# Finer input loads, identity matmuls and tied weight splits at the first norm, and three re-ordered places behind it

## The chip, the cores and the metric

The kernel runs on one core of a Trainium2 chip. The time is the device time of one execution in microseconds (us); lower is better. The core's engines take instructions from queues of their own, each in order: PE (TensorE, matmuls, with its weight loads shown as PEld), DVE (VectorE), ACT (ScalarE), POOL (GpSimd) and SP (SyncE, which here only issues DMAs). Engines wait for each other by semaphores. The profile also gives the clock that PE was granted (PEclk; 1.00 is full, 0.50 half).

## The reference

640 frames (one prompt of 512, eight streams of 16 new frames) of 1024 channels go through two layers and a final RMSNorm, all in fp32. Layer 0, where nearly all of the change lies, is:

```python
def conv_module(h, hist, g, w_pw1, b_pw1, w_dw, b_dw, ln_g, ln_b, w_pw2, b_pw2):
    a, gate = jnp.split(rms_norm(h, g) @ w_pw1 + b_pw1, 2, axis=-1)
    glu = a * jax.nn.sigmoid(gate)
    full = jnp.concatenate([hist.astype(glu.dtype), glu], axis=1)
    y = depthwise_conv(full, w_dw) + b_dw          # causal, width 31
    y = jax.nn.silu(layer_norm(y, ln_g, ln_b))
    return h + y @ w_pw2 + b_pw2, full[:, -30:]

def swiglu_ffn(h, g, w_in, w_out):
    a, b = jnp.split(rms_norm(h, g) @ w_in, 2, axis=-1)
    return h + (jax.nn.silu(a) * b) @ w_out
```

Layer 1 is chunked attention over 16 heads instead of the convolution, then another FFN of the same form. The last 30 rows of `full` are outputs too.

## The kernel before

Channels lie on the 128 partitions in 8 tiles (k = 0..7), frames along the free dimension in two groups g0 and g1 of 320. Every fp32 product is made of three matmuls on operands split in a high and a low part: `mm3` (L179 to L185) issues wh·xh (L182), wl·xh (L183) and wh·xl (L184). A weight block of 128x2048 is loaded into `raw` (L144, on SP), ACT makes the high part `whi` (L155), DVE or POOL the low part `wlo` (L159). Activations are split by `xsplit`: `xh` on ACT (L171), `xl` on DVE (L172).

A norm squares 8 tiles (L191 on ACT, L194 elsewhere), adds them in order (`acc`, L212), reduces over partitions with a matmul against a column of ones (the mean, L221), adds eps (DVE, `rst`, L255), takes the power -1/2 on POOL (L262), and spreads the row over the partitions with a matmul against the identity matrix (L233). DVE then scales each tile (`n`, L277).

The stages, by time in the profile: first RMSNorm and the pointwise products of the convolution layer with the gate `glu` (L726 to L739) and the depthwise taps, up to 159 us; of the taps some run on DVE (L778), some on ACT and POOL (L785, L788), and some on PE (L832) from copies of a channel tile that are written to DRAM (`sa`, `sb`, L808) and read back shifted (`xa`, `xb`, L814). Then LayerNorm (`conv_ln`, per group: mean, spread, subtract L851, squares and adds L867, spread, scale L883), the product `pw2` with the update of `h` (L924), FFN0 from about 260 us, attention, FFN1 from about 1043 us, final norm.

A scheduler of the framework sets each engine's order from priorities (`high_priority`) and from explicit ties (`tc.issue_after`: not ahead of that instruction). The order of the convolution stage is written out in the string `PLAN` (L69): a letter for a step, a digit for a channel tile; `E7`/`F7` are the products of tile 7 for g0 and g1, `S7 A7` its taps on PE for the first part, `n` the LayerNorm of g0 between the last taps, `m w0 w1` the LayerNorm of g1 and the two `pw2`. `HELD` says how many DVE taps are held back at which step.

In the FFN, seven products of sums stand in for eight (`seven`), with operands `XH`/`XL` per combination (L342, L343). `std` does the first three products plainly, its second half with `XT4` and `X22`, which need the norm of the second half of the frames (`stats(1)`).

Of the kernel before, what the change touches and what calls it, by code (L numbers as in the profile page):

```python
# [15 lines left out]
P = 128  # L16
# [9 lines left out]
SB = 16  # L26
# [10 lines left out]
MEAN_AT, SPREAD_AT, STATS1_AT = 3, 5, 2  # L37
# [7 lines left out]
GAPS = 1, 12, 2  # L45
# [6 lines left out]
C01 = 4  # L52
# [4 lines left out]
SSQ = 'avavavav'  # L57
# [11 lines left out]
SSQ1 = 'ppapappp'  # L69
LNO = ((0, 1, 4, 5, 6, 2, 3, 7), (0, 1, 4, 2, 3, 5, 6, 7))  # L70
PLAN = ("a0 y x1 b0 b1 q0 dp1s0 c2 k ds1p2 D3 C4 S3 q3 ds2 C5 E6 S4 A4 F6 B4 E7 e S5 A5 F7 k k k S6 A6 "
        "S7 A7 n s0 m w0 w1")

HELD = {(1, 0): 21, (2, 0): 9}
# [7 lines left out]
def tile_trunk(ctx, tc, xT, vecs, hist, w_pw1, w_pw2, w_in0, w_out0, w_os0, w_in1, w_out1, w_os1,  # L82
# [28 lines left out]

    def load_x(g):
# [20 lines left out]
    def wsplit(src, k, n, parts=1, pool=0, cuts=1, gains=None):  # L133
# [6 lines left out]
        else:  # L140
            src = src if len(src.shape) == 2 else src.rearrange("p m c -> p (m c)")
            for i in range(cuts):
                a, b = sz * i // cuts, sz * (i + 1) // cuts
                nc.sync.dma_start(raw[:, a:b], src[:, a:b])  # L144
# [7 lines left out]
        with tc.high_priority(offset=HP):  # L152
            for i in range(cuts):
                a, b = sz * i // cuts, sz * (i + 1) // cuts
                nc.scalar.activation(out=hi[:, a:b], in_=raw[:, a:b], func=AF.Copy)  # L155
                c = b - (b - a) * pool // 4
                for eng, a, b in ((nc.vector, a, c), (nc.gpsimd, c, b)):
                    if a < b:
                        eng.tensor_tensor(out=lo[:, a:b], in0=raw[:, a:b],  # L159
                                          in1=hi[:, a:b].bitcast(F32), op=ALU.subtract)  # L160
        return hi, lo

    @contextmanager
    def behind(*ins):
        with ExitStack() as st:
            for i in ins:
                st.enter_context(tc.issue_after(i))
            yield

    def xsplit(src, hi, lo):  # L170
        split_end[0] = nc.scalar.activation(out=hi, in_=src, func=AF.Copy).ins  # L171
        nc.vector.tensor_tensor(out=lo, in0=src, in1=hi.bitcast(F32), op=ALU.subtract)  # L172
# [14 lines left out]
    def square(s, n, eng="a", q=None):  # L187
        if q is None:
            q = tp.tile([P, tw[0]], F32, tag=sqt[0], name=nm("sq"))
        if eng == "a":  # L190
            nc.scalar.activation(out=q[:, :n], in_=s, func=AF.Square)  # L191
# [10 lines left out]
    def colmean(st, pieces, n, cut, tag, eng=nc.gpsimd, accp=None):  # L202
# [3 lines left out]
        for s in pieces[:cut]:  # L206
# [5 lines left out]
            eng.tensor_tensor(out=acc[:, :n], in0=prev, in1=s(), op=ALU.add)  # L212
# [17 lines left out]

    def spread(st, r, n, ins=False):
        for t, a in enumerate(tiles(n)):
            end = nc.tensor.matmul(st[:, a:a + P], r[:, t:t + 1].to_broadcast([P, P]), ident,  # L233
                                   start=True, stop=True)
        return end.ins if ins else st[:, :n]
# [12 lines left out]
    def rstd_bc(pieces, n, engs=SQ, cut=CUT, r2=None, eng=nc.gpsimd, newton=False,  # L248
                accp=None, sqs=None):
# [3 lines left out]
                         for i, (s, e) in enumerate(zip(pieces, engs))], n,  # L253
                       cut, "rst", eng, accp)
        nc.vector.tensor_scalar(out=r[:, :nt], in0=v, scalar1=EPS, scalar2=None,  # L255
                                op0=ALU.add)
# [4 lines left out]
        else:  # L261
            nc.gpsimd.tensor_tensor(out=r2[:, :nt], in0=r[:, :nt], in1=mhalf[:, :nt], op=ALU.pow)  # L262
# [6 lines left out]
    def rms(g, gain, engs=SQ, cut=CUT, eng=nc.gpsimd, hold=None):  # L269
        n = gr[g][1]  # L270
        bc, _ = rstd_bc([hp(g, k) for k in range(KT)], n, engs, cut, None, eng,
                        accp=hold and hold())
        xh, xl = new_xs(g)
        for k in range(KT):
            t = hold() if hold and k < 2 else tp.tile([P, tw[0]], F32, tag="n1", name=nm("n1"),
                                                       bufs=NB1)
            nc.vector.scalar_tensor_tensor(out=t[:, :n], in0=hp(g, k), scalar=col(gain, k),  # L277
                                           in1=bc, op0=ALU.mult, op1=ALU.mult)
# [25 lines left out]
    def ffn(l, w_in, w_out, w_os, tail, hf, lead=(), b0=None):  # L304
# [1210 lines left out]
```

## Time and profile before

| | us |
|---|---|
| median of 3 runs (lowest, highest) | 1488.08 (1486.97, 1489.66) |
| profiled execution | 1485.55 |
| its span from first to last instruction | 1483.6 |
| PE busy | 1429.4 (96%) |
| DVE busy | 1138.3 (77%) |
| ACT busy | 757.2 (51%) |
| PE idle until the first mean (L221) | 12.3 |
| PE idle for `xa` of tile 7 (L832) | 6.1 |

The span is 1.95 us shorter than the time of its execution, and that execution 2.5 us shorter than the median. Idle time of PE is what a change of order can take away; the page's list of waits names, for each, the instruction that waited and the one that released it. A matmul's printed time includes the end of its pipeline; what a stream of them costs is read from start to start.

### The profile page before, as it was taken

Reading aid. Unit: us, or ns where it says so; the run is one execution under the profiler, and the core shown is the slowest. Engines: PE = TensorE matmul, PEld = TensorE weight load, DVE = VectorE, ACT = ScalarE, POOL = GpSimd, SP = SyncE. Lnnn points to the kernel's source line nnn. Section 1 sums busy time; section 2 is a strip of 40 time slices with the busy share of each in tenths; the row PEclk is TensorE's granted clock in tenths of the full one; section 3 lists DMA queues with packets and bytes.
Section 4 is the critical chain, followed back from the end, with each engine's and each line's share of the span. In section 5 each row is a group of like instructions: output and inputs, shape, how many; then the busy total and the mean of one; then the engine's idle time right before and its main releaser. Section 6 shows DMA issues by size and latency. Waiting matters only on the chain.

```text
span 1483.6 us, 28030 instructions
## 1 busy us (share of the span) xinstructions
PE 1429.4 (96%) x10932; PEld 1365.9 (92%) x10932; DVE 1138.3 (77%) x2523; ACT 757.2 (51%) x1620; POOL 297.7 (20%) x356
## 2 busy tenths in 40 slices
PE   5999899999999999999999999999999999999997
PEld 5998699999999999999988888987899999999997
DVE  5789656799888888866766767566799888888755
ACT  3666245465454564445655454443565455455443
POOL 5789102001111111103222112010001111111101
PEclk9999999999999999999999999999999999999999
DMA  7256514125445444433655555361224444544512
GB/s 239 68 160 189 138 58 136 36 75 143 131 116 133 134 118 130 132 109 133 212 164 204 180 173 193 129 208 23 86 75 129 138 118 117 150 118 108 153 64 72
DMA packets 66660, 192.56 MB, mean 130 GB/s; under 512 B 12000, under 2 KB 30176, under 8 KB 58080
## 3 DMA queue, kind: packets, MB, share of 16 engines
q1 hardware_dynamic: 52736, 161.10, 33.5%
q0 software_dynamic: 13504, 29.37, 9.7%
q8 instruction: 86, 1.41, 0.4%
q14 instruction: 46, 0.38, 0.1%
q10 hardware_dynamic: 288, 0.31, 0.1%
HBM read 179.14 MB, written 11.61 MB: 129 GB/s over the span
## 4 chain that ended last, share of the span: by engine, by line
PE 77%; DVE 8%; POOL 6%; ACT 3%; DMA 3%; issue 3%; SPq 0%; POOLq 0%; DVEq 0%; ACTq 0%
PE mm L409 46%; PE mm L182 8%; PE mm L183 7%; PE mm L184 7%; POOL ca L788 5%; PE am L1226 1%; PE am L1209 1%; PE w L221 1%; PE w L1242 1%; ACT whi L147 1%; PE am L1273 1%; DVE wlo L343 1%; PE mm L832 1%; DVE B L446 1%; PE w L1185 1%
## 5 line engine op out<-in xcount | busy, mean ns | idle before, releaser
L409 PE MATMUL mm<-XH,wlo 128*128 128x320 f32 x896 | 276.9, 310 | 0.0
L409 PE MATMUL mm<-XH,whi 128*128 128x320 f32 x896 | 276.1, 311 | 0.7 <-ACT t L419 0.5
L409 PE MATMUL mm<-XL,whi 128*128 128x320 f32 x896 | 274.4, 310 | 0.0
L342 ACT ACTIVATE whi<-raw 128x512 fp32r<-128x512 f32 (+2 forms) x280 | 169.2, 614 | 141.3 <-PE mm L409 116.5
L182 PE MATMUL mm<-xh,whi 128*128 128x320 f32 (+2 forms) x640 | 202.5, 318 | 6.4 <-ACT xh L171 4.2
L343 DVE TENSOR_TENSOR wlo<-raw,whi 128x512 fp32r<-128x512 f32 (+2 forms) x280 | 184.9, 668 | 22.4 <-ACT whi L342 21.0
L183 PE MATMUL mm<-xh,wlo 128*128 128x320 f32 (+2 forms) x640 | 201.1, 315 | 0.6 <-DVE wlo L159 0.6
L184 PE MATMUL mm<-xl,whi 128*128 128x320 f32 (+2 forms) x640 | 198.4, 313 | 0.0
L409 PE MATMUL mm<-hid,whi 128*128 128x320 f32 x732 | 171.4, 310 | 2.2 <-DVE hid L343 2.2
L409 PEld LDWEIGHTS mm<-XH,whi 128*128 128x128 f32 x896 | 168.4, 189 | 2.1 <-ACT t L419 1.3
L409 PEld LDWEIGHTS mm<-XH,wlo 128*128 128x128 f32 x896 | 169.0, 189 | 0.0
L409 PEld LDWEIGHTS mm<-XL,whi 128*128 128x128 f32 x896 | 167.9, 188 | 0.0
L182 PEld LDWEIGHTS mm<-xh,whi 128*128 128x128 f32 x640 | 122.5, 192 | 9.7 <-ACT xh L171 5.0
L409 PEld LDWEIGHTS mm<-hid,whi 128*128 128x128 f32 x732 | 124.8, 188 | 4.2 <-DVE hid L343 3.2
L183 PEld LDWEIGHTS mm<-xh,wlo 128*128 128x128 f32 x640 | 122.9, 192 | 1.0 <-DVE wlo L159 0.8
L184 PEld LDWEIGHTS mm<-xl,whi 128*128 128x128 f32 x640 | 121.8, 191 | 0.4 <-issue 0.2
L409 PE MATMUL mm<-hid,wlo 128*128 128x320 f32 x366 | 112.9, 308 | 0.0
L409 PE MATMUL mm<-XL,shi 128*128 128x320 f32 x344 | 105.5, 308 | 5.0 <-DVE XL L343 5.0
L409 PE MATMUL mm<-XH,shi 128*128 128x320 f32 x344 | 105.8, 308 | 0.7 <-ACT XH L342 0.7
L409 PE MATMUL mm<-XH,slo 128*128 128x320 f32 x344 | 105.7, 307 | 0.0
L388 POOL DMA_DIRECT2D s<-in_w_in x38 | 22.1, 581 | 386.2 <-DVE wlo L343 207.9
L788 POOL TENSOR_TENSOR ca<-ca,cvt 128x512 f32<-128x512 f32 x60 | 91.7, 1528 | 15.0 <-ACT cvt L785 8.0
(255 smaller groups left out, 3345.2 us busy)
## 6 DMA issues: line engine op xcount, KB each, us to landing
raw<-in_w_in SPq DMA_DIRECT2D x38, 1024.0 KB
s<-in_w_in POOLq DMA_DIRECT2D x76, 256.0 KB, 4.2
raw<-in_w_os SPq DMA_DIRECT2D x24, 768.0 KB
cache<-in_ck SPq DMA_DIRECT2D x32, 512.0 KB
cache<-in_cv SPq DMA_DIRECT2D x32, 512.0 KB
raw<-in_w_pw SPq DMA_DIRECT2D x12, 1024.0 KB
s<-in_w_os POOLq DMA_DIRECT2D x48, 192.0 KB, 3.6
raw<-in_w_kq SPq DMA_DIRECT2D x8, 1024.0 KB
```

Of the source, the lines that this page charges most:

```text
L147: nc.scalar.activation(out=hi[:, a:b], in_=raw[:, a:b], func=AF.Copy, scale=gain)
L182: nc.tensor.matmul(ps, wh, xh, start=(first and i == 0), stop=False)
L183: nc.tensor.matmul(ps, wl, xh, start=False, stop=False)
L184: end = nc.tensor.matmul(ps, wh, xl, start=False, stop=(stop and i == last))
L221: mean_end[0] = nc.tensor.matmul(st[:, 512 + t * w + k:513 + t * w + k], s[:, a:a + P], onec, start=True, stop=True).ins
L342: put_end[1] = nc.scalar.activation(out=hi, in_=src, func=AF.Copy).ins
L343: put_end[0] = nc.vector.tensor_tensor(out=lo, in0=src, in1=hi.bitcast(F32), op=sub).ins
L388: nc.gpsimd.dma_start(s1, src[:, 2 * n:3 * n])
L409: last = nc.tensor.matmul(pt, wt, v, start=(first and k == i == 0), stop=(k == n - 1 and i == 2), skip_group_check=True)
L446: nc.vector.scalar_tensor_tensor(out=out, in0=x, scalar=-1.0, in1=y, op0=mult, op1=op)
L788: nc.gpsimd.tensor_tensor(out=acc, in0=acc, in1=pr, op=ALU.add)
L832: conv_end[0] = nc.tensor.matmul(pt[32 * q:32 * q + 32, 0:n], w4[0:r, 4 * tg + q, :], mv, start=(tg == 0), stop=(tg == 7)).ins
```

## The change

At the first norm: the two loads of the first 320 frames become four of two channel tiles each, and so do those of the second; the weight loads of the first tile are put behind the last of them. `warm(n)` issues n matmuls of the 128x128 identity by itself into a product tile: 30 at the start (nothing but `ident` is waited for), 9 behind the mean, 5 behind the spread of g0 and 5 behind that of g1. The splits of the first two weight blocks are tied behind the last square, the last add, `rst`, `pow` or a scaled tile. The last square goes from DVE to ACT; the squares of g1 go all to ACT. The split of weight block 2 is made in two halves.

At the end of the convolution: the store of `sa` stands ahead of the copy to `out_convs`; the second `pw2` block is loaded early, the split of the first is made late (token `f`); the read of `xb` of tile 6 is put behind that of `xa` of tile 7; fewer DVE taps run before F7, the rest behind it. The LayerNorm of g1 is interleaved with the parts of `pw2` of g0 (`GAPS1`).

In the FFNs: the squares of `stats` get eight tiles of their own in place of two rotating ones; in FFN1 the third plain product's second half stands behind the spread, and `stats(1)` is tied one step earlier. At the end of attention the mean and the spread of FFN1's first half stand one half-product later (`MEAN_AT`, `SPREAD_AT`).

PE at the start of the program, before; `w` is the tile of the mean and the spread, `mm` are product tiles, `ident` the identity:

```order
1 L221 MATMUL w_4_119<-onec,acc_122 128x1 x3
2 L233 MATMUL w_4_119<-ident,rst_15_149 128x128 x3
3 L182 MATMUL mm_209<-xh_154,whi_105 128x320
4 L183 MATMUL mm_209<-xh_154,wlo_106 128x320
5 L182 MATMUL mm_234<-xh_154,whi_105 128x320
6 L183 MATMUL mm_234<-xh_154,wlo_106 128x320
7 L182 MATMUL mm_268<-xh_154,whi_190 128x320
```

and of the changed kernel:

```order
1 L145 MATMUL mm_106<-ident 128x128 x30
2 L237 MATMUL w_2_137<-onec,acc_140 128x1 x3
3 L145 MATMUL mm_169<-ident 128x128 x9
4 L251 MATMUL w_2_137<-ident,rst_13_167 128x128 x3
5 L145 MATMUL mm_199<-ident 128x128 x5
6 L198 MATMUL mm_258<-xh_197,whi_180 128x320
7 L199 MATMUL mm_258<-xh_197,wlo_181 128x320
```

Four groups of `ident` products (the fourth is further down, behind the second spread) now stand around the mean and the spread.

SP at the end of the convolution before, from the store of `sb` of tile 6 (`raw` is a weight block of `pw2`):

```order
55 L808 DMA sb_1566<-gall 128x350
56 L144 DMA raw_2403<-in_w_pw 128x2048
57 L814 DMA xb_1568<-sb_1566 32x4x350
58 L814 DMA xb_1568<-sb_1566 32x4x349
59 L814 DMA xb_1568<-sb_1566 32x4x348
60 L814 DMA xb_1568<-sb_1566 32x4x347
61 L957 DMA out_convs<-gall 128x368
62 L808 DMA sa_1672<-gall 128x590
63 L814 DMA xa_1674<-sa_1672 32x4x590
```

and of the changed kernel, from that store:

```order
54 L846 DMA sb_1631<-gall 128x350
55 L846 DMA sa_1726<-gall 128x590
56 L1015 DMA out_convs<-gall 128x368
57 L852 DMA xa_1728<-sa_1726 32x4x590
58 L852 DMA xa_1728<-sa_1726 32x4x589
59 L852 DMA xa_1728<-sa_1726 32x4x588
60 L852 DMA xa_1728<-sa_1726 32x4x587
61 L852 DMA xb_1733<-sb_1631 32x4x350
```

The store of `sa` of tile 7 moved from behind the weight load, the four `xb` reads and `out_convs` to directly behind the store of `sb`, and its reads stand ahead of those of `xb`; the weight load went further ahead.

DVE between the taps and the sums of the LayerNorm of g0, before (`w` are taps, `gall` the gate's output, `y` the convolution's result):

```order
216 L778 SCALAR_TENSOR_TENSOR w_113_789<-gall,dwv,w_113_789 128x128
217 L778 SCALAR_TENSOR_TENSOR w_174_1225<-gall,dwv,w_174_1225 128x128 x13
218 L739 SCALAR_TENSOR_TENSOR gall<-t_226_1836,t_227_1838 128x320
219 L159 TENSOR_TENSOR wlo_2347<-raw_2345,whi_2346 128x2048
220 L212 TENSOR_TENSOR acc_1986<-y_102 128x320
221 L212 TENSOR_TENSOR acc_1986<-acc_1986,y_102 128x320 x5
222 L225 TENSOR_REDUCE mst_1999<-w_233_1985 128x3
```

and of the changed kernel:

```order
215 L816 SCALAR_TENSOR_TENSOR w_178_1285<-gall,dwv,w_178_1285 128x128 x5
216 L777 SCALAR_TENSOR_TENSOR gall<-t_233_1887,t_234_1889 128x320
217 L816 SCALAR_TENSOR_TENSOR w_178_1285<-gall,dwv,w_178_1285 128x128 x4
218 L179 TENSOR_TENSOR wlo_1494<-raw_1492,whi_1493 128x2048
219 L816 SCALAR_TENSOR_TENSOR w_178_1285<-gall,dwv,w_178_1285 128x128 x9
220 L228 TENSOR_TENSOR acc_2052<-y_104 128x320
221 L228 TENSOR_TENSOR acc_2052<-acc_2052,y_104 128x320 x5
222 L241 TENSOR_REDUCE mst_2065<-w_240_2051 128x3
```

Thirteen taps moved behind the last gate, and with them the sums stand 13 taps later in DVE's work behind that gate.

PE in FFN0 around the spread of the second half (`XH`, `XL` are operands, `whi`, `wlo` the weight halves), before:

```order
1320 L409 MATMUL mm_3088<-XH_316_2764,whi_2783 128x320
1321 L409 MATMUL mm_3088<-XH_316_2764,wlo_2784 128x320
1322 L233 MATMUL w_362_2940<-ident,rst_373_2975 128x128 x3
1323 L409 MATMUL mm_3088<-XL_317_2765,whi_2783 128x320
1324 L409 MATMUL mm_3089<-XH_316_2764,whi_2783 128x320
1325 L409 MATMUL mm_3089<-XH_316_2764,wlo_2784 128x320
```

and of the changed kernel:

```order
1304 L435 MATMUL mm_3133<-XH_318_2822,wlo_2844 128x320
1305 L435 MATMUL mm_3133<-XL_319_2823,whi_2843 128x320
1306 L251 MATMUL w_358_2992<-ident,rst_361_3019 128x128 x3
1307 L435 MATMUL mm_3133<-XH_318_2822,whi_2843 128x320
1308 L435 MATMUL mm_3133<-XH_318_2822,wlo_2844 128x320
1309 L435 MATMUL mm_3133<-XL_319_2823,whi_2843 128x320
1310 L435 MATMUL mm_3133<-XH_318_2822,whi_2843 128x320
1311 L435 MATMUL mm_3133<-XH_318_2822,wlo_2844 128x320
1312 L435 MATMUL mm_3133<-XL_319_2823,whi_2843 128x320
1313 L435 MATMUL mm_3132<-XH_320_2824,whi_2843 128x320
```

Behind the spread stood 13 products up to the first one of the second half (`mm_3183` with `XH_310`); now 30 stand there.

The diff, cut to its core:

```diff
-MEAN_AT, SPREAD_AT, STATS1_AT = 3, 5, 2
+MEAN_AT, SPREAD_AT, STATS1_AT = 4, 6, 1
-GAPS = 1, 12, 2
+GAPS, GAPS1 = (1, 12, 2), (5, 3, 10, 4)
-SSQ = 'avavavav'
+SSQ = 'avavavaa'
-SSQ1 = 'ppapappp'
-LNO = ((0, 1, 4, 5, 6, 2, 3, 7), (0, 1, 4, 2, 3, 5, 6, 7))
+SSQ1 = 'aaaaaaaa'
+WARM = 30, 9, 5, 5
+LNO = ((0, 1, 4, 5, 6, 3, 2, 7), (0, 1, 4, 2, 3, 5, 6, 7))
-HELD = {(1, 0): 21, (2, 0): 9}
+HELD, HELD2 = {(1, 0): 21, (2, 0): 4}, {(2, 0): 14}
...
-        for k in range(0, KT, 4):
-            nc.sync.dma_start(h[:, k:k + 4, g0:g0 + n], xT[g][:, k:k + 4, :])
+        for k in range(0, KT, 2):
+            norm_end["x"] = nc.sync.dma_start(h[:, k:k + 2, g0:g0 + n], xT[g][:, k:k + 2, :]).ins
...
+    def warm(n):
+        pt = mmt()
+        for _ in range(n):
+            end = nc.tensor.matmul(pt[:, 0:P], ident, ident, start=True, stop=True)
+        return end.ins
...
+        if WARM[2 + g]:
+            with behind(norm_spread[0]):
+                warm(WARM[2 + g])
...
-        def std(ws, half, sink):
+        def std(ws, half, sink, second=None):
...
-                xproduct(pa, ws[k], x, k == 0)
-                ends.append(xproduct(pb, ws[2 + k], x, k == 0).ins)
+                with tc.issue_after(second) if k and second else nullcontext():
+                    xproduct(pa, ws[k], x, k == 0)
+                    ends.append(xproduct(pb, ws[2 + k], x, k == 0).ins)
...
-                            (nc.gpsimd, nc.vector)[half], half == 1)
+                            (nc.gpsimd, nc.vector)[half], half == 1, sqs=x12 + x22)
...
-    w00 = wsplit(w_pw1[0], 16, P, cuts=4, pool=PL1[0])
-    with tc.high_priority(offset=2 * HP):
-        xs = [rms(0, V_NCONV, SSQ, SCUT, nc.vector), None]
+    def first():
+        with behind(mean_end[0]):
+            warm(WARM[1])
+        pws[0] = wsplit(w_pw1[0], 16, P, cuts=4, pool=PL1[0],
+                        ties=[(norm_end["sq"], norm_end[e]) for e in ("acc", "acc", "rst", "rst")])
+
+    with tc.issue_after(warm(WARM[0])), tc.high_priority(offset=2 * HP):
+        xs = [rms(0, V_NCONV, SSQ, SCUT, nc.vector, hook=first), None]
+    pws[1] = wsplit(w_pw1[1], 16, P, cuts=4, pool=PL1[1],
+                    ties=(norm_end["sq"], norm_end["n"][3], norm_end["pow"]))
...
-            w = pws.get(c) or wsplit(w_pw1[c], 16, P, pool=PL1[c])
+            w = pws.get(c) or wsplit(w_pw1[c], 16, P, pool=PL1[c], cuts=2)
...
+                read = conv_shift(c, "a", 0, NSC if op == "D" else NXA, True)
+                if c + 2 == KT:
+                    pws[KT, 0] = wsplit(w_pw2[0], 16, P, late=True)
+                    with tc.issue_after(store_end[0]):
+                        pws[KT, 1] = wsplit(w_pw2[1], 16, P)
+                x4s[c] = [w4, read(), None]
+                if c + 1 == KT:
+                    with tc.issue_after(read_end[0]):
+                        x4s[c - 1][2] = x4s[c - 1][2]()
+                with tc.issue_after(store_end[0]):
+                    nc.sync.dma_start(convs_out[:, c], gs[:, c])
...
+        elif op == "f":
+            with behind(gate_end[0], glu_end[0]):
+                conv_taps(held, {})
+                pws[KT, 0] = pws[KT, 0]()
...
-            for _ in conv_ln(1, sum_end[0]):
+            ln, products = conv_ln(1, sum_end[0]), pw2(0, zs[0])
+            for gap in GAPS1:
+                for _ in range(gap):
+                    with tc.issue_after(conv_end[0]):
+                        next(products)
+                with tc.issue_after(conv_end[0]):
+                    next(ln, None)
+            while next(products, 0) is None:
                 pass
```

More of the change, by code (lines that the diff above doesn't have):

```diff
@@ L51 @@
 SQ = 'aaaaaaaa'
-C01 = 4
 NB1 = 2
@@ L143, in wsplit @@
                 a, b = sz * i // cuts, sz * (i + 1) // cuts
-                nc.sync.dma_start(raw[:, a:b], src[:, a:b])
+                with behind(norm_end["x"]) if cuts > 2 else nullcontext():
+                    nc.sync.dma_start(raw[:, a:b], src[:, a:b])
         if gains is not None:
```

147 lines of the change are left out of this document (86 added, 61 removed).

## The prediction

> **What bounds the kernel now.** First the page's busy shares, then the waits of PE (engine, line, what it waited for: total, times, longest):
>
> ```profile
> PE 1429.4 (96%) x10932; PEld 1365.9 (92%) x10932; DVE 1138.3 (77%) x2523; ACT 757.2 (51%) x1620; POOL 297.7 (20%) x356
> PE w L221 <- DVE acc L212: 12.3, 1, 12.3
> PE mm L409 <- DVE XL L343: 5.0, 3, 2.2
> PE mm L182 <- ACT xh L171: 4.2, 3, 1.6
> PE w L233 <- POOL rst L262: 2.9, 2, 1.6
> PE mm L182 <- ACT t L726: 1.2, 1, 1.2
> PE w L1364 <- DVE sqs L1357: 1.0, 1, 1.0
> PE mm L183 <- DVE wlo L159: 0.6, 1, 0.6
> ```
>
> PE is the bound, so only its idle and half-speed stretches can go. With the 6.13 for `xa` quoted below the change touches some 30 us of waits; but a wait is gained only as far as nothing else is late next, and the 12.3 are mostly the input's landing. The places follow in order of time.
>
> The start, by the timeline of PE, ACT and DVE (start, duration, instruction), PE's busy time in a window, and line L233's durations (least, median, most):
>
> ```profile
> 7.67 0.47 ACT L191 ACTIVATE sq<-h 128x320 f32<-128x320 f32 x1 [0.91 <-DMA h<-in_xa]
> 10.50 1.29 DVE L159 TENSOR_TENSOR wlo<-raw,whi 128x512 fp32r<-128x512 f32 x2
> 11.70 0.48 DVE L212 TENSOR_TENSOR acc<-acc,sq 128x320 f32<-128x320 f32 x1
> 12.33 1.41 PE L221 MATMUL w<-onec,acc 128*128 128x1 f32 x6 [12.33 <-DVE acc L212]
> 15.38 1.65 PE L233 MATMUL w<-ident,rst 128*128 128x128 f32 x6 [1.63 <-POOL rst L262]
> L233 PE MATMUL w<-ident,rst x52: 270/275/581, 15.4 to 1476.2; 128*128 128x128 f32 x52
> 18.16 0.63 PE L182 MATMUL mm<-xh,whi 128*128 128x320 f32 x1 [1.14 <-ACT xh L171]
> 18.20:23.50 5.30, 5.30 (x20) 5.30 (x21) 5.15 (x9) 2.42 (x7) 4.24 (x5) 1.00 0.94 192
> 31.82 0.31 PE L183 MATMUL mm<-xh,wlo 128*128 128x320 f32 x1
> 31.97 0.31 PE L184 MATMUL mm<-xl,whi 128*128 128x320 f32 x1
> 32.12 0.72 PE L221 MATMUL w<-onec,w 128*128 128x1 f32 x6
> 37.76 0.41 PE L182 MATMUL mm<-xh,whi 128*128 128x320 f32 x1 [1.50 <-ACT xh L171]
> ```
>
> The last input lands at 7.67, but the last add is at 11.70, behind two `wlo` and a square on DVE. From 18.20 to 23.50 PE runs 20 products at 5.30/20 = 0.265; later ones start 0.147 apart. So the clock was half for 5.3 us after the first product (the window's 1.00 has no clock record behind it), and 20 x 0.118 = 2.4 us went there.
>
> **Start, -3.1.** Six records of a spread stand for three matmuls. Cold they take 1.65 with a last one of 0.58: (1.65-0.58)/5 = 0.214 each; the warm spread at 282.37, quoted below, takes 0.83 with 0.275: 0.111. Thirty identity matmuls are 60 records. From 1.65 (`ident` done on POOL, by the start of PE's work an estimate) and with the clock lifted 5.3 us later, as above, 25 are cold and 35 warm: the run ends at 6.95 + 3.9 = 10.9. Data is ready earlier: with `wlo` tied behind the adds, DVE needs after 7.67 a square on ACT (0.47) and two adds of 0.5: about 9.3. So the run itself is what the mean waits for. Mean 10.9 to 11.6 (0.72 as at 32.12), nine identities (18 x 0.111 = 2.0, over the 1.63 for `rst` and the power), spread 0.83, five identities 1.1 (the 1.14 to `xh`): first product at 15.5 in place of 18.16, -2.7, then 20 products at full speed, -2.4. Against that: `wlo` now comes behind the adds and `rst`, between the `n` and `xl`: four products' pieces at 0.65 each, of which I let 1.0 show; and the second norm. There the mean and spread stand directly behind each other (1.6 of waiting, which before had 18 products in it) with 1.1 of identities, +2.7; 24 products now cover the 1.50 at 37.76, -1.5; and the first product lasts 0.41 as at 37.76, not 0.63, -0.2. Sum -2.7 - 2.4 + 1.0 + 2.7 - 1.5 - 0.2 = -3.1. Bounds: the run ends at 9.4 and no `wlo` shows, -5.6; +4.5 in the first rival.
>
> The Trainium skill, "TensorE: Matmul & The Clock Gate", Part 1: the gate opens about 4 us into sustained activity, in a free-running window of 3.4. By it the run would end at some 10.2 (an estimate) and the term would be -3.8. The row's 5.3 is taken.
>
> **Splits in halves, -0.8.** The waits of 0.6 (`wlo`) and 1.2 (`t`): two halves give the first products their `wlo` half a split earlier, so most of 0.6; the 1.2 depends on the order of ACT, 0 to 1.2.
>
> **Tile 7 of the convolution, -5.6.** SP's, PE's and DVE's timelines:
>
> ```profile
> 148.29 1.74 SPq L814 DMA_DIRECT2D xb<-sb  x4
> 151.42 0.38 SPq L808 DMA_DIRECT2D sa<-gall  x1
> 156.05 3.47 SPq L814 DMA_DIRECT2D xa<-sa  x4
> 155.02 4.57 PE L832 MATMUL mm<-xa,w 128*32 128x128 f32 x128
> 165.72 6.77 PE L832 MATMUL mm<-xa,w 128*32 128x128 f32 x128 [6.13 <-DMA xa<-sa]
> 172.43 0.83 PE L221 MATMUL w<-onec,acc 128*128 128x1 f32 x6
> 163.50:170.30 6.80, 4.58 (x80) 4.31 (x84) 0.00 (x0) 0.37 (x1) 0.00 (x0) 0.50 0.77 176
> 147.38 9.96 DVE L778 SCALAR_TENSOR_TENSOR w<-gall,dwv,w 128x128 f32<-128x128 f32 x32
> 157.65 2.29 DVE L159 TENSOR_TENSOR wlo<-raw,whi 128x2048 fp32r<-128x2048 f32 x1
> 160.37 2.67 DVE L212 TENSOR_TENSOR acc<-acc,y 128x320 f32<-128x320 f32 x5
> ```
>
> The data of the store is there at 147.4, when DVE's taps resume, but SP issues it at 151.42, behind the `xb` reads and a copy; the reads follow at 156.05, their data at 165.72. The change issues the store some 4 us earlier, with no `xb` reads beside it, so its reads go out at 151 to 152 and end, at the same 9.7 us, at 157 to 161; PE comes there at 159.6. The 6.13 go, and the half clock that followed (6.77 against 4.57, 2.2). The mean could then stand at 164.9, 7.5 earlier, but DVE is late next: behind the gate (157.25 to 157.65) come now 4 taps, `wlo`, 9 taps and 6 sums, 13 x 0.311 (9.96/32) + 2.29 + 3.15 (the row at 160.37 and one sum ahead of it) = 9.5 behind 157.65, ending at 167.1, or at 165.8 if the gate, with fewer taps ahead, comes 1.3 earlier. I take 166.8: 172.43 - 166.8 = 5.6. Bounds: -7.5, and -3 if the reads end at 162.
>
> **LayerNorm of g1 inside `pw2`, 0.** The timelines of PE and DVE, and the half-clock stretches of this part and FFN0 by windows:
>
> ```profile
> 227.08 0.41 PE L182 MATMUL mm<-xh,whi 128*128 128x320 f32 x1 [1.58 <-ACT xh L171]
> 228.40:231.70 3.30, 2.96 (x11) 2.96 (x12) 2.38 (x6) 3.30 (x9) 0.00 (x0) 0.50 0.00 0
> 224.95 3.27 DVE L883 TENSOR_TENSOR y<-y,w 128x320 f32<-128x320 f32 x8 [2.90 <-PE w L233]
> 282.37 0.83 PE L233 MATMUL w<-ident,rst 128*128 128x128 f32 x6
> 288.76 0.41 PE L409 MATMUL mm<-XL,shi 128*128 128x320 f32 x1 [2.19 <-DVE XL L343]
> 289.80:293.20 3.40, 3.40 (x15) 3.40 (x14) 3.40 (x10) 0.68 (x2) 0.00 (x0) 0.50 0.00 0
> 1068.88 0.41 PE L409 MATMUL mm<-XH,shi 128*128 128x320 f32 x1 [0.73 <-ACT XH L342]
> 1073.22 0.41 PE L409 MATMUL mm<-XL,shi 128*128 128x320 f32 x1 [2.04 <-DVE XL L343]
> 1044.72 1.69 DVE L343 TENSOR_TENSOR XL<-hid,XH 128x320 fp32r<-128x320 f32 x4
> 1045.26 0.41 PE L409 MATMUL mm<-XL,shi 128*128 128x320 f32 x1
> ```
>
> Sixty products now cover the 1.58 and the half clock (3.4 us at half cost 1.7): -3.3. But between this norm's first spread and its mean stand 60 products, 60 x 0.147 = 8.8, and DVE has there eight subtractions (3.27, as at 224.95), two `wlo` of 2.29 (as at 157.65), eight adds of 0.45 (2.67/6 a piece) and two updates of `h` of the same: 3.27 + 4.58 + 3.6 + 0.9 = 12.4. A new wait of 3.6 would arise, less what DVE does ahead: I take 3.3, net 0. Bounds -4 (no wait) and +2.3 (wait with its own half clock).
>
> **FFN0, -3.2.** Seventeen products, 2.5 us, more between the spread at 282.37 and the products that wait 2.19 for `XL`; the chain behind the spread (eight scalings, sums, `XL`) starts when ACT has copied it, so it moves whole. The half clock of 3.4 at 289.80 (1.7) follows that wait; -3.9 together. I take -2.9 and -0.3 for another `XL` wait of 0.7. Bounds -4.5, 0.
>
> By the Trainium skill, same page and section, the clock returns to half after an idle window of about 3.4 us. Here it did after 2.19; by the page this term would be -2.2 alone, the sum 1 less.
>
> **End of attention, -0.2.** The 1.0 at the mean (`sqs`) goes, but the spread stands six products later, and there PE already takes `XL` at 1045.26, just as DVE has it (1044.72 + 0.49): that wait takes the place of the first.
>
> **FFN1, -2.4.** 0.73 + 2.04 at 1068.88 and 1073.22; the spread stands 20 products, 2.9 us, earlier. Bounds -2.8, 0.
>
> Sum: -3.1 - 0.8 - 5.6 + 0 - 3.2 - 0.2 - 2.4 = -15.3 against the profiled 1485.55, which lies 2.5 below the median; from the median: 1488.08 - 15.3 = 1472.8.
>
> **Rivals.**
> 1. The identity matmuls don't lift the clock (what they are is thinner than a product: 128 columns, not 320). The run ends at 1.65 + 60 x 0.214 = 14.5, mean 1.41, nine 3.9, spread 1.65, five 2.1: first product at 23.5, 5.3 late, less 0.8 gained at the second norm: +4.5, total 1480.4. For it: no row shows such a run at the start; against it: nothing in the row of 5.3 us suggests that width counts. 0.08.
> 2. The waits only move: DVE's taps hold the mean of g0 to 169 (-3), g1's mean waits and its clock halves (+2.3), FFN0 gains its wait alone (-2.2), the start 1 less: -3.1 + 1 - 0.8 - 3 + 2.3 - 2.2 - 0.2 - 2.4 = -8.4, total 1479.7. For it: 77% of DVE busy, and every one of these places has it late next. 0.22.
> 3. Slower. ACT's split of the second `pw2` block now stands ahead of tile 6's gate, and waits for a load of 1 MB that is put between `sa` stores and reads. Each us it lands behind about 142 holds ACT, then the product tiles, then PE. It has 11 us from its issue; to outweigh 15.3 it would have to land after 157. The longest that a step of SP's DMAs there takes is the 9.7 us of the `xa` reads, so two such would have to lie ahead of it. If it lands at 160, the total is 1488.1 - 15.3 + 18 = 1490.8, and more with the half clock behind the stall. 0.05.
> 4. Little changes: the gains at the start and in the FFNs are met by waits of like size; within 0.2% (3 us, about what a measurement of this kernel can tell from no change). 0.05.
>
> The forecast has 0.60. Cases 1 and 2 are faster too: 0.90 in all, less 0.02 for a mixture with 4; same 0.06, slower 0.06. The lower bounds together (-5.6 - 1.8 - 7.5 - 4 - 4.5 - 0.9 - 2.8) are -27.1; two thirds of the way there from the sum is -23, 1465. Upwards the range takes in rivals 1 and 2: 1482.
>
> **What would show it.** Right: first mean near 11, first product near 15.5, products 0.147 apart from the first; no wait for `xa`; mean of g0 some 5.6 earlier relative to the end of F7; no half clock near 290; no wait over 1 us for `XL` in the FFNs. Wrong: identity rows 0.21 apart to the end; a wait for `acc` or `y` in the LayerNorms of 3 us and more with a half clock behind it; ACT idle for `raw` near 142.

## The result and the profile after

The changed kernel takes 1477.26 us (median of 4 executions, 1475.63 to 1478.7), the kernel before 1488.87: a ratio of 0.9923, interval 0.9906 to 0.9940, 11.6 us less. In a second set of executions, against 1487.21, it was 0.9928 (0.9914 to 0.9942). The forecast was 15.3 less, range 6 to 23. The two profiled executions lie closer together than the medians: 1477.64 (span 1475.5) against 1485.55 (span 1483.6), since that of before was 3.3 below its median. The account below is of these two, so it has to explain 8.1 us of span.

PE's waits in the changed kernel (the list has the same columns as before):

```profile
PE w L237 <- DVE acc L905: 4.3, 2, 3.6
...
PE w L251 <- POOL rst L281: 2.5, 2, 1.3
PE mm L198 <- ACT t L764: 2.1, 1, 2.1
PE mm L870 <- issue: 1.9, 1, 1.9
PE mm L145 <- POOL ident masks.py:199: 1.6, 1, 1.6
PE w L1434 <- DVE sqs L1427: 1.6, 1, 1.6
...
PE mm L435 <- DVE XL L369: 0.6, 1, 0.6
```

The 12.3 us before the first mean, the 6.1 for `xa` and the 5.0 for `XL` are gone or down to 0.6. Four waits are new or longer: 3.6 for `acc` (L905, the mean of the LayerNorm of g1), 2.1 for `t` (L764, the gate's activation), 1.9 with no releaser in the taps (L870), 1.6 for `sqs`.

Where the time went is read by places that both traces have. The start of PE's work there, by PE's timeline, in us ("near its end" is the last product of an FFN ahead of its last wait):

| place | before | after | lead | gained in the stretch | forecast |
|---|---|---|---|---|---|
| first product of g0 | 18.16 | 15.39 | 2.8 | 2.8 | |
| first product of g1 | 37.76 | 36.12 | 1.6 | -1.1 | 3.1 to here |
| taps at 118 us | 118.40 | 115.73 | 2.7 | 1.0 | 0.8 |
| taps of tiles 6 and 7 | 155.02 | 154.58 | 0.4 | -2.2 | 0 |
| first mean of the LayerNorm of g0 | 172.43 | 166.05 | 6.4 | 5.9 | 5.6 |
| FFN0's first product | 260.15 | 255.24 | 4.9 | -1.5 | 0 |
| FFN0 near its end | 655.59 | 646.64 | 9.0 | 4.0 | 3.2 |
| last products of attention | 1024.70 | 1015.78 | 8.9 | 0 | |
| FFN1's first product | 1043.63 | 1036.51 | 7.1 | -1.8 | 0.2 |
| FFN1 near its end | 1437.31 | 1429.04 | 8.3 | 1.2 | 2.4 |

The rows at the places that gain, by PE's timeline of the changed kernel:

```profile
1.62 9.28 PE L145 MATMUL mm<-ident 128*128 128x128 f32 x60 [1.62 <-POOL ident masks.py:199]
10.74 0.73 PE L237 MATMUL w<-onec,acc 128*128 128x1 f32 x6
13.42 0.83 PE L251 MATMUL w<-ident,rst 128*128 128x128 f32 x6
15.39 0.41 PE L198 MATMUL mm<-xh,whi 128*128 128x320 f32 x1
15.64 0.31 PE L199 MATMUL mm<-xh,wlo 128*128 128x320 f32 x1
15.79 0.31 PE L198 MATMUL mm<-xh,whi 128*128 128x320 f32 x1
...
154.58 7.60 PE L870 MATMUL mm<-xa,w 128*32 128x128 f32 x221
164.07 1.82 PE L870 MATMUL mm<-xa,w 128*32 128x192 f32 x35 [1.89 <-issue]
166.05 0.83 PE L237 MATMUL w<-onec,acc 128*128 128x1 f32 x6 [0.16 <-DVE acc L228]
...
1063.45 0.42 PE L435 MATMUL mm<-XL,shi 128*128 128x320 f32 x1 [0.57 <-DVE XL L369]
```

The run of 60 records ends at 10.9, and from the first product on they start 0.147 apart: the clock is up.

And those that lose (PE, at 120 us ACT, and at 1027 us DVE), each followed by a stretch at half clock, which the windows show (PEclk is the number ahead of the last two):

```profile
29.14 0.93 PE L251 MATMUL w<-ident,rst 128*128 128x128 f32 x6 [1.20 <-POOL rst L281]
117.57 1.32 ACT L823 ACTIVATE cvt<-gall,dwv 128x512 f32<-128x512 f32 x2
121.22 0.72 ACT L823 ACTIVATE cvt<-gall,dwv 128x512 f32<-128x512 f32 x1 [2.32 <-POOL ca L826]
121.85 0.51 ACT L764 ACTIVATE t<-mm,hb 128x320 f32<-128x320 f32 x1
122.41 0.53 PE L198 MATMUL mm<-xh,whi 128*128 128x320 f32 x1 [2.11 <-ACT t L764]
207.54 1.14 PE L237 MATMUL w<-onec,acc 128*128 128x1 f32 x6 [3.60 <-DVE acc L905]
1027.05 1.22 DVE L369 TENSOR_TENSOR wlo<-raw,whi 128x1024 fp32r<-128x1024 f32 x1
1029.92 0.94 PE L1434 MATMUL w<-onec,sqs 128*128 128x1 f32 x6 [1.56 <-DVE sqs L1427]
```

```profile
30.50:33.80 3.30, 3.30 (x16) 3.30 (x15) 3.30 (x7) 1.84 (x4) 1.75 (x2) 0.50 0.71 283
122.70:126.00 3.30, 3.30 (x14) 3.30 (x14) 0.90 (x4) 2.44 (x4) 3.14 (x3) 0.51 0.58 143
208.00:214.70 6.70, 6.70 (x27) 6.70 (x27) 0.71 (x2) 0.00 (x0) 0.85 (x1) 0.50 0.34 141
1030.60:1033.90 3.30, 3.30 (x14) 3.30 (x14) 1.56 (x3) 0.00 (x0) 0.88 (x1) 0.50 0.62 165
```

Between the start and the final norm the kernel before had 17.1 us at half clock (163.5 to 170.3 and three stretches of 3.4); the changed one has 17.1 too, in other places. At the start itself the half clock fell from 5.3 us of products to none. In a second profiled execution of the changed kernel (the run "The changed kernel again" below) the stretch at 30.4 was missing and one at 167.1 stood in its place; the others lay behind the same waits.

### The profile page after: what moved, and what is told of

It reads as the page before. It is cut to its first block, busy times and chain, and to the rows that moved or that the text cites. A ratio compares the mean times of both kernels' runs of the same rounds, so it can differ in the third digit from the quotient of the medians.

```text
span 1475.5 us, 28228 instructions
## 1 busy us (share of the span) xinstructions
PE 1440.5 (98%) x11030; PEld 1377.4 (93%) x11030; DVE 1140.7 (77%) x2523; ACT 756.6 (51%) x1628; POOL 293.1 (20%) x350
## 4 chain that ended last, share of the span: by engine, by line
PE 73%; DVE 10%; POOL 6%; DMA 5%; issue 3%; ACT 3%; POOLq 0%; SPq 0%; DVEq 0%; ACTq 0%
PE mm L435 41%; PE mm L198 8%; PE mm L200 7%; PE mm L199 7%; POOL ca L826 5%; DMA raw<-in_w_in 3%; DVE wlo L369 1%; DMA raw<-in_w_os 1%; PE am L1296 1%; PE w L1312 1%; PE w L237 1%; PE am L1279 1%; ACT whi L163 1%; PE am L1343 1%; DVE h L572 1%
```

## The experiments

Each ratio is to the kernel before on the same chip. The changed kernel stands at 0.9923 and 0.9928. It ran beside the four kernels from "The changed kernel again" to "Three edits together", not beside the others, which are held against it by their ratios. Where two intervals overlap, as they do for differences under some 0.002, the times don't tell the kernels apart, and the reading is from the profiles.

**The first norm alone.** The edits of the first norm, with the rest as before, and weight block 2 split whole as before: the constants are

```diff
-SSQ = 'avavavav'
-SSQ1 = 'ppapappp'
+SSQ = 'avavavaa'
+SSQ1 = 'aaaaaaaa'
+WARM = 30, 9, 5, 5
```

> The kernel before with the first norm's part of the change alone (loads, identity matmuls, tied splits, squares, gate ties); all else as before. In the changed kernel 2.7 us of lead at 118 us shrank to 0.5 at 123, behind a wait of 2.1 us for ACT. Theory A (the lead is real; it was lost to the order of ACT that the other parts brought about there, a third tap conversion ahead of the gate's activation): the lead of 2.7 at 118 is still 2 or more when the taps of tile 7 wait for their data; total 2 to 3 us below the kernel before, about 1486. Rival B (POOL's chain of taps sets the pace, and takes back any lead whatever the order): 2.7 at 118, under 0.8 at 131, total within 1 us of before. Rival C (the identity matmuls don't lift the clock): first product after 20 us, slower than before.

1485.77 against 1485.89, ratio 1.0001 (0.9989 to 1.0013). The first product was at 15.22, the lead at 118 us 3.7, at the taps of tiles 6 and 7 3.1 (151.94 for 155.02). So C falls, and B as it was put. A holds up to there, since the lead was 2 or more, but its total didn't come. The wait for `xa` grew to 7.06, and the mean behind it (170.73) led by 1.7:

```profile
163.57 7.23 PE L870 MATMUL mm<-xa,w 128*32 128x128 f32 x128 [7.06 <-DMA xa<-sa]
```

At FFN1's first product this profile led by 3.1 still, at its last by 0.9, with a half-clock stretch in between (1070.2 to 1073.6). Tile 7 took back 1.4 of the 3.1: 0.9 in the longer wait, the rest in a half clock that lasted 10.2 us in place of 6.8. What is left is of the size that the clock's stretches give and take. By the interval the start is worth between 1.6 us and a loss of 1.9 by itself, not 3.1.

**LayerNorm of g1 ahead of the products again.**

```diff
-            for gap in GAPS1:
-                for _ in range(gap):
-                    with tc.issue_after(conv_end[0]):
-                        next(products)
-                with tc.issue_after(conv_end[0]):
-                    next(ln, None)
+            for _ in ln:
+                pass
```

> The changed kernel with the LayerNorm of g1 finished ahead of the products of g0, as before the change. In the changed kernel the stretch from the first of these products to FFN0's first product took 70.8 us, before it 67.3. Theory A (the interleaving brought a wait of 3.6 us before that norm's mean and two half-clock stretches): the stretch is back at 67 to 68 us, and the total 2 to 3.5 us below the changed kernel, about 1474.5. Rival B (the moved weight loads and the earlier LayerNorm of g0 cost it, not the order): 70 us or more, total as the changed kernel, 1477.

The stretch was 184.91 to 251.40, 66.5 (A). The total, 0.9929 (0.9915 to 0.9943), is not below the changed kernel's; the profiled span is, by 2.6 (1472.9). A stands for the place, and the total is open within the interval.

**No identity matmuls behind the second spread.** `WARM = 30, 9, 5, 0`.

> The changed kernel without the five identity matmuls behind the second spread. With them the first products have three accumulators in place of four, and the second mean and spread stand directly behind each other; a half-clock stretch of 3.4 us followed at 31. Theory A (these five cost more than they give): nine products stand between mean and spread again, no half clock near 31, the first product of g1 at 33.5 in place of 35.0; total 1 to 2 below the changed kernel, about 1475.5. Rival B (they keep the clock up): a wait of 1.1 to 1.5 us before the first product of g1 and a half-clock stretch behind it, total the same or 1 to 2 more.

```profile
32.66 0.42 PE L198 MATMUL mm<-xh,whi 128*128 128x320 f32 x1 [1.14 <-ACT xh L186]
117.44 0.41 PE L198 MATMUL mm<-xh,whi 128*128 128x320 f32 x1
154.14 3.58 PE L870 MATMUL mm<-xa,w 128*32 128x128 f32 x103 [1.11 <-DMA xa<-sa]
158.95 1.33 PE L870 MATMUL mm<-xa,w 128*32 128x192 f32 x25 [1.23 <-issue]
161.11 0.83 PE L237 MATMUL w<-onec,acc 128*128 128x1 f32 x6 [0.84 <-DVE acc L228]
```

Eight products stand between mean and spread, g1 begins at 32.66 in place of 36.12, and the wait near 118 is gone too, since ACT has two conversions instead of three ahead of that activation: at the taps of tiles 6 and 7 (148.46) the lead on the changed kernel was 6.1. There three waits of 1.1, 1.2 and 0.8 and 6.8 us of half clock behind them (from 161.9) took back more than half of it (181.92 against 184.49 at the first product of `pw2`), a stretch of 3.4 at 189.2 more, and at FFN0's first product 1.1 was left. The total is the same, 0.9937 (0.9921 to 0.9953): A at its own place, wrong in the sum.

**84 products between spread and mean of the LayerNorm of g1.** `GAPS1 = (5, 3, 14, 4)`.

> The changed kernel with 84 products in place of 60 between the first spread of the LayerNorm of g1 and its mean (14 parts for 10 in the third place). Theory A (PE waits there because DVE's chain of about 12.4 us is longer than 60 products, 8.8 us): 84 products are 12.3 us, so the wait of 3.6 us falls under 0.5 and the half clock behind it goes; the stretch to FFN0 is 65 to 67 us, total 3 to 5 below the changed kernel, about 1473. Rival B (DVE's chain itself moves back with the products, since updates of h stand in it): a wait of 2 us or more stays there or before the next spread; total 1476 to 1478.

```profile
210.25 0.83 PE L237 MATMUL w<-onec,acc 128*128 128x1 f32 x6 [0.42 <-DVE acc L905]
```

The wait fell from 3.60 to 0.42 and no half clock followed; the stretch was 185.30 to 251.33, 66.0, against 70.8. Total 0.9908 (0.9892 to 0.9924), 1472.45, 2.8 below the earlier LayerNorm order and 4.9 below the kernel without the five identities, on the same chip. A at its place: the cause of that wait is shown, DVE's chain was longer than the products. Against the changed kernel the total is 0.0015 to 0.002 lower by the ratios, which the times just don't tell. In this profile no half clock followed the wait of 1.55 at the end of attention (1028.59) either, so not all of the shorter span is the edit's.

**The changed kernel again,** without an edit, as the measure for the next three.

> The changed kernel once more, so that the next ones stand beside it on one chip. Its profile shows, if the account holds in a second execution: wait of about 2.1 us for ACT near 120, of 1.4 to 1.9 us with no releaser in the taps of tile 7, of 3.6 us before the second mean of the LayerNorm of g1, of 1.6 us at the end of attention. Half-clock stretches may lie behind other waits than in the first execution, if their windows run free of the program. About 10 to 12 us below the kernel before.

1475.92, ratio 0.9928, 11.3 below. Waits of 2.1 (`t`), 1.4 (no releaser), 3.6 and 1.6 (`sqs`): as expected.

**Mean and spread at the end of attention in their old place.** `MEAN_AT, SPREAD_AT = 3, 5`.

> The changed kernel with mean and spread at the end of attention where they stood before the change. In the changed kernel PE waits 1.6 us there, since a weight split (1.22 us) and two updates of h stand ahead of the last sum on DVE, and half the clock follows for 3.4 us. Theory A (the later place brought the split ahead of the sum): wait of 1.0 again, no half clock, the stretch from the attention's last products to FFN1's first 1.5 to 2 us shorter, total 1 to 2 below the changed kernel. Rival B (the wait only depends on DVE's load): wait 1.6 to 2.4, total the same or slower by up to 1.

```profile
1025.16 0.83 PE L1434 MATMUL w<-onec,sqs 128*128 128x1 f32 x6 [0.98 <-DVE sqs L1427]
```

The wait was 0.98, no half clock followed, and from the product near FFN0's end to FFN1's first 388.1 us passed in place of 389.9. A at its place. The times, 1474.79 against 1475.92 (0.9920, 0.9905 to 0.9936), agree with it and don't prove it.

**The FFN's statistics as before.**

```diff
-                            (nc.gpsimd, nc.vector)[half], half == 1, sqs=x12 + x22)
+                            (nc.gpsimd, nc.vector)[half], half == 1)
...
-            with nullcontext() if b0 is None else tc.issue_after(put_end[0]):
+            with tc.issue_after(put_end[0]):
```

with `std` and `STATS1_AT` as before. The tie is the one that the changed kernel lacks in FFN0; in FFN1 it has it too.

> The changed kernel with the FFN's statistics as before: two rotating tiles for the squares, the tie of the second tiles in FFN1, no tie of the third product's second half, one step later. Theory A (the earlier spread took the waits for XL away): the waits of 2.2 us near 280 and of 2.0 near 1063 and a half clock in FFN0 are back, total 4 to 5.5 above the changed kernel. Rival B (FFN0's gain comes from the earlier stages' timing): under 2 us more.

```profile
284.58 0.41 PE L435 MATMUL mm<-XL,shi 128*128 128x320 f32 x1 [2.21 <-DVE XL L369]
1069.32 0.41 PE L435 MATMUL mm<-XL,shi 128*128 128x320 f32 x1 [1.11 <-DVE XL L369]
```

1481.47, ratio 0.9962 (0.9947 to 0.9976), 5.5 above the changed kernel; the wait in FFN0 is back. In FFN1 there are three waits, of 0.59 for `XH`, 0.94 for `hid` and 1.11 for `XL`, in place of the one of 2.0, and FFN0 had no half clock behind its wait here. A by its total and by the wait in FFN0; the half clock and the one wait in FFN1 did not come. The two profiled executions differ by 3.2 us only (1481.47 and 1478.31, the slowest of its kernel), so some 2 of the 5.5 are not traced.

**Three edits together:** no five identities, 84 products, old place at the end of attention.

> The changed kernel without the five identity matmuls behind the second spread, with 84 products between spread and mean of the LayerNorm of g1, and with mean and spread at the end of attention as before the change. Theory A (each of the three was a separate loss): first product of g1 at 32.7, no wait near 118, wait before the mean of g1 under 1 us, total 5 to 8 below the changed kernel. Rival B (leads ahead of the taps of tile 7 and of the LayerNorm are taken back there by data and DVE): the lead at 148 of some 6 us is 2 or less at FFN0's first product beyond what the 84 products give; total 3 to 4.5 below the changed kernel.

PE's waits:

```profile
PE mm L435 <- DVE hid L369: 3.7, 6, 1.0
PE mm L435 <- DVE XL L369: 1.7, 3, 0.6
PE mm L145 <- POOL ident masks.py:199: 1.6, 1, 1.6
PE w L251 <- POOL rst L281: 1.3, 1, 1.3
...
PE mm L870 <- issue: 1.2, 1, 1.2
```

1468.64, ratio 0.9874 (0.9857 to 0.9891), 7.3 below the changed kernel on the same chip: A, and the lowest time measured here. No wait for `t` at 118 and none for `acc` or `sqs` of over 1 us is left. At FFN0's first product it stood at 246.46 (the changed kernel 255.42), with 6.8 us at half clock up to the final norm in place of 17.1. Of these 9.0 the 84 products give 4.8, so B falls. How much of the 10 us less of half clock is the edits' and how much this execution's is not separated.

**The end of the convolution as before.** The taps, the token `f`, the store and read order and the early `pw2` split go back; the tie of the other `pw2` loads behind the last `xb` reads stays.

```diff
-HELD, HELD2 = {(1, 0): 21, (2, 0): 4}, {(2, 0): 14}
+HELD = {(1, 0): 21, (2, 0): 9}
...
-                read = conv_shift(c, "a", 0, NSC if op == "D" else NXA, True)
-                if c + 2 == KT:
-                    pws[KT, 0] = wsplit(w_pw2[0], 16, P, late=True)
-                    with tc.issue_after(store_end[0]):
-                        pws[KT, 1] = wsplit(w_pw2[1], 16, P)
-                x4s[c] = [w4, read(), None]
+                x4s[c] = [w4, conv_shift(c, "a", 0, NSC if op == "D" else NXA), None]
```

> The changed kernel with the order at the end of the convolution as before: the store of tile 7 behind the reads of tile 6's xb and the copy out, the taps not held back behind the last gate, the first weight block of pw2 split early. Theory A (this order took the wait for xa away): PE waits 6 to 7.5 us for xa again, the first mean of the LayerNorm stands 5 to 7 later, and the total is 4 to 7 above the changed kernel. Rival B (DVE's chain behind the gate, which is the next late one, is worth as much): the mean moves by under 3, total up by under 2.5.

A was wrong, and B by its reason: the mean moved by 2.2, but forward. SP's and PE's timelines, first of the kernel before (those that the prediction doesn't show), then of this one:

```profile
141.94 0.38 SPq L808 DMA_DIRECT2D sb<-gall  x1
144.57 0.35 SPq L144 DMA_DIRECT2D raw<-in_w_pw  x1
160.81 0.82 SPq L144 DMA_DIRECT2D raw<-in_w_pw  x1
...
141.97 3.45 SPq L852 DMA_DIRECT2D xb<-sb  x4
145.95 0.36 SPq L1008 DMA_DIRECT2D out_convs<-gall  x1
147.94 0.34 SPq L846 DMA_DIRECT2D sa<-gall  x1
150.86 1.74 SPq L852 DMA_DIRECT2D xa<-sa  x4
...
155.00 8.93 PE L870 MATMUL mm<-xa,w 128*32 128x128 f32 x256
163.87 0.83 PE L237 MATMUL w<-onec,acc 128*128 128x1 f32 x6
...
185.93 0.64 PE L198 MATMUL mm<-xh,whi 128*128 128x320 f32 x1 [3.55 <-ACT xh L186]
```

The store of tile 7 stands behind the `xb` reads and the copy, as in the kernel before, and yet no wait for `xa` is left, and the mean comes 2.2 earlier than in the changed kernel. So the order of stores and reads alone does not make that wait. What differs from the kernel before is that no weight load of 1 MB is among these DMAs (there one was issued at 144.57, another at 160.81 beside the `xa` reads): the `xb` reads went out 2.0 us behind the store of `sb`, not 6.4, and the reads of `xa` 2.9 behind their store, not 4.6. The loads are the likely cause; a kernel with the loads in place and the new order, which would part the two, was not run. The held-back taps, for their part, cost 2.2 at the mean, or 2.6 from the taps' start on (8.9 us in place of 11.5).

The total is 0.9944 (0.9929 to 0.9959), not told apart from the changed kernel's. What the earlier mean gained was lost again, since now the `pw2` weights are late: 3.55 of waiting at 185.93 and 6.8 us of half clock.

**No identity matmuls at all.** `WARM = 0, 0, 0, 0`.

> The changed kernel without any identity matmuls at its norms (none at the start, behind the mean or behind the spreads). Theory A (the identities lift the clock, but the group behind the second spread takes back as much as they give): first mean at 10.0, first product at 15.5 to 16.5, products 0.267 apart for some 5 us, first product of g1 at 34.5 to 36 (35.0 with them); total within 1.5 of the changed kernel. Rival B (the finer loads and tied splits alone do it, the clock being lifted by the products soon): first product of g1 at 33 or below, total lower. Rival C (the identities carry the start): first product of g1 at 37 or above, total 2 or more higher.

```profile
10.97 1.41 PE L237 MATMUL w<-onec,acc 128*128 128x1 f32 x6 [10.97 <-DVE acc L228]
16.77 0.64 PE L198 MATMUL mm<-xh,whi 128*128 128x320 f32 x1 [1.14 <-ACT xh L186]
17.20 0.47 PE L199 MATMUL mm<-xh,wlo 128*128 128x320 f32 x1
17.47 0.47 PE L198 MATMUL mm<-xh,whi 128*128 128x320 f32 x1
```

Products 0.267 apart, the first of g1 at 35.61, between the 36.12 and 34.72 of the changed kernel's two executions; ratio 0.9938 (0.9924 to 0.9951), the same within the intervals. The first mean and product came 1.0 and 0.3 later than put; for the rest A: in this form the identities lift the clock and give nothing in the end. Without them the third conversion on ACT did not come either, and at the taps of tiles 6 and 7 PE led the changed kernel by 3.2 (151.42); at FFN0's first product it was 1.2 behind (256.44). The kernel with 30, 9 and 5 but without the last five reached 32.66 at that place.

**The `xb` reads of tile 6 behind the last store,** in the changed kernel and in the fastest one:

```diff
-                if c + 1 == KT:
-                    with tc.issue_after(read_end[0]):
-                        x4s[c - 1][2] = x4s[c - 1][2]()
...
+                    if c + 1 == KT:
+                        with tc.issue_after(store_end[0]):
+                            x4s[c - 1][2] = x4s[c - 1][2]()
```

> The changed kernel with the reads of xb of tile 6 behind the last store, so that they don't follow the reads of xa of tile 7 at once. In five kernels PE stood 1.2 to 1.9 us in the taps of tile 7 with no releaser, and went on 1.4 to 1.6 us after a packet of 16 KB on an instruction queue had ended, which took 1.2 to 1.5 us beside full DMA engines. Theory A (PE waits for its instructions, and they for the full engines): with the engines emptier when that packet is fetched, it takes under 0.8 us and the wait falls by 0.5 to 1.5; total down by no more than 1. Rival B (the fetch is late for another reason): the wait stays at 1.2 to 1.9.

> The same move of the xb reads in the kernel without the five identities, with 84 products and with the old place of mean and spread at the end of attention. If the wait without a releaser shrinks there too: 0.5 to 1.5 below that kernel, 13 times 1.4 per mille under the kernel before (ratio 0.986 to 0.987). If not, or if xb is late for the taps in its turn: ratio 0.987 to 0.989.

```profile
157.79 4.56 PE L870 MATMUL mm<-xa,w 128*32 128x128 f32 x128 [0.52 <-ACT y L785]
164.58 0.83 PE L237 MATMUL w<-onec,acc 128*128 128x1 f32 x6 [2.23 <-DVE acc L228]
```

(The rows are those of the first of the two.) The wait with no releaser was gone in both, but PE then waited for DVE's sums, 2.23 and 2.12, in one piece, and 6.8 us of half clock followed: 0.9959 (0.9947 to 0.9971), slower than the changed kernel; in the other 0.9891 (0.9875 to 0.9906), the same as without the move. No forecast of these two runs came: A had the total down, B the wait as before, and the second run a ratio of 0.987 at most where the wait goes. The packet took 1.24 us, not under 0.8, with the DMA engines full meanwhile, against 1.20 in the changed kernel with a share of 0.69: that speaks against A's mechanism (a fetch that full engines draw out). What changed is its time, 156.49 in place of 161.30; the wait does depend on this order. The runs do settle what bounds the mean there: without that wait it stood 11.9 us behind the taps' start, with it 11.5, so DVE's sums set it.

## Why the prediction was right, and where it was off

The direction, the range and the case were right; the size was a third too large (15.3 for 11.6), outside the interval of the measurement, and the time lies between the forecast and rival 2 (1479.7), in which "the waits only move". Between the two profiled executions the gain by the places is 8.3, about the 8.4 of rival 2's sum, though not by its places: tile 7 and FFN0 gave what the forecast had. So part of the nearness to the forecast is luck, the 3.3 us by which the profiled execution of the kernel before lay under its median. By its steps:

- **Start, -3.1:** its first half came out as put (run to 10.9, first product at 15.4 for 15.5), with some luck: in the twelve profiles with the run of 30 the clock was lifted between 4.9 and 7.9 us, where 6.95 was taken, and the first product stood between 14.7 and 16.1. What was left out of the term is the half clock behind the second norm's mean, wait and spread: with it the lead at g1 was 1.6, without it, in the second profile, 3.0. And the step said nothing on what the lead meets further on: a third conversion on ACT ahead of the gate's activation (2.2 lost at 120), tile 7 (1.4 lost in the kernel with the start alone). Measured alone the start gave nothing that times can tell.
- **Splits in halves, -0.8:** 1.0 gained up to 118, but not by the halves: the wait for `wlo` is gone as well in the kernel with the first norm alone, which splits that block whole, 5.4 us earlier than before (45.32 for 50.71). The wait for `t` went from 1.2 to 2.1 and took a half clock with it. "Depends on the order of ACT, 0 to 1.2" had no bound on the side of a loss, and that cost 2.2. The wait of 2.1 stands in all eight profiles that have the five last identities and the halves, and in none of the five changed ones that lack one of the two; which of them calls the third conversion forward is open.
- **Tile 7, -5.6:** 5.9 measured; DVE's chain behind the gate was late next, as put. The mean at 166.05 for the 166.8 taken is no second proof: with the leads of the two steps ahead it should have stood at 162.9. The reason given for the late data, "behind the `xb` reads and a copy", does not suffice: in that order but without weight loads among these DMAs no wait was left. (The bound of -7.5 should be -8.3 by its own terms, 6.13 and 2.2.)
- **LayerNorm of g1, 0:** the new wait was 3.6 as worked out (3.3 taken), and came with its own half clock of 6.8 us, which only the bound of +2.3 took in. A stretch of 3.4 at 194.2 in the kernel before, which the step doesn't name, was gone. Measured +1.5; with 84 products instead of 60 the new wait goes.
- **FFN0, -3.2:** 4.0; the wait and the half clock are gone, and so is the other wait for `XL`, of 0.74 at 262.23, of which the step took 0.3. Putting the statistics back costs 5.5 with FFN1's.
- **End of attention, -0.2:** a loss of 1.8. The step asked what is late next behind the spread, not what the later place does to the sums ahead of the mean: a weight split of 1.22 us came ahead of the last ones on DVE (1027.05; before, it stood behind them, at 1037.85), the wait grew to 1.56, and half a clock followed.
- **FFN1, -2.4:** 1.2; 0.57 of the wait for `XL` stayed, and waits of 0.37 for `h` (1037.73) and 0.58 for ACT's `hid` (1127.86) are new.

Rival 1 is refuted: the clock was up from 6.5 us on, within the run of identities, whose records start 0.111 apart from there. Rival 3 did not occur: ACT's split of the second `pw2` block ran at 138.44, with its load long there. On the clock, the rule of the Trainium skill ("TensorE: Matmul & The Clock Gate", Part 1) that about 3.4 us of idling bring it back to half is not what these traces show: it fell behind waits of 1.56 (1029.92) and 2.11 (122.41). An estimate by that rule would have had no half clock in the changed kernel between start and final norm but behind the 3.60.

## What to carry to other kernels

On an engine that is busy 96% of the time, a lead won at the start is worth only what the next bound by data or by another engine lets through; price the meeting places (here ACT's in-order queue and DMA landing) before adding up terms. A wait of 1.2 to 2.2 us on PE can cost as much again in clock: 1.7 us for each stretch of 3.4 at half. Whether one long wait is worse than several short ones is not shown: 2.2 in one piece was followed by 6.8 us at half, and so were 1.1, 1.2 and 0.8 in the kernel without the last five identities. Extra matmuls that keep the clock up have to be priced like any other work: the five behind the second spread put g1's first product 2.1 to 3.5 us later, and the total was none the better for them.

## What was not expected of the hardware

In nine of the fourteen profiles PE stood 1.2 to 1.9 us in the taps of tile 7 with no semaphore to wait for, and went on 1.4 to 1.6 us after the end of a packet of 16 KB on the instruction queue (in the changed kernel 161.30 to 162.50, PE on again at 164.07; in the fastest one 156.10 to 157.45 and 159.01). Such packets took 1.0 to 1.3 us also with the DMA engines otherwise idle (in the changed kernel at 142.40, 165.58 and 172.59), and up to 1.7 beside other transfers. In the two kernels with the `xb` reads moved and in the one with the old end of the convolution PE went through; in the kernel before and in the one with the first norm alone it waited for `xa` instead. That it waits for its own instructions there is the likely reading, and not shown; what makes the fetch late is open.

Between the start and the final norm the clock's half stretches last 3.41 us or a multiple in every profile, and which short waits bring them on depends on the execution. Nine profiles have a wait of 1.2 us before the second spread; a stretch followed in five of them and none in four. The wait of 1.55 at the end of attention stands in nine; one followed in seven and none in two (84 products, no identities). Each such stretch is worth 1.7 us, which is more than several of the edits are.
